# One of four weight sums of a seven-product multiplication moved from accumulating transfers to GpSimd, and two pieces of work swapped in the first set

## The chip, the core and the metric

One core of one Trainium2 chip runs the whole program in one launch. The metric is device time in microseconds of one execution, median of three runs.

## What is computed

A two-layer decoder trunk on 256 tokens of width 1024. Each layer has two feed-forward parts around a token mixer and a cross-attention; everything is float32:

```python
def swiglu(h, w_gate, w_up, w_down):
    return (jax.nn.silu(h @ w_gate) * (h @ w_up)) @ w_down

for i in range(DEPTH):                      # DEPTH = 2
    h = h + 0.5 * swiglu(rmsnorm(h, ffn1_norm[i]), ffn1_w_gate[i], ffn1_w_up[i], ffn1_w_down[i])
    ...                                     # mixer, cross-attention
    h = h + 0.5 * swiglu(rmsnorm(h, ffn2_norm[i]), ffn2_w_gate[i], ffn2_w_up[i], ffn2_w_down[i])
```

The gate and up matrices are 1024 x 2816, so a feed-forward part works through five and a half blocks of 512 hidden columns. The change is in the first feed-forward part of the program, `ffn1` of layer 0.

## The kernel before

**Precision.** TensorE multiplies in a reduced float32. Each weight is therefore split into a high part (`whi`, a cast on ScalarE, L224) and a low part (`wlo`, weight minus high part, a subtraction on VectorE, L225), and each block of a product is three matmuls: high by high, low by high, high by low (`mm3`, L262, L263, L264). The unit of this work is a *granule* (class `Gran`): two weight blocks of 128 rows x 512 columns, so each split is one 128x1024 instruction on ScalarE and one on VectorE. There are four buffers for high and four for low parts, so the splits can stand at most four granules ahead of TensorE. The low part is first wanted by the second matmul of its granule (L263).

**Seven products.** For some column blocks, gate and up are computed together: with B11, B21 the upper and lower 512 rows of the up block and B12, B22 those of the gate block, a 2x2 block product is done with seven block products in place of eight (`seven`). This needs sums of weights as right operands:

- X1 = B11 + B12, into a tile of its own, by VectorE (L203);
- X2 = X1 + B22, in place, by VectorE (L203, a 128x2048 addition of two SBUF tiles);
- X4 = X2 + B21, in place, by two transfers issued by GpSimd that read B21 from memory again and add it to the tile (L199);
- X3 = B12 + B22, in place over B12, before the change by two such transfers too.

The products come in the order B11, X1, X2, B22, X3, B21, X4; each is two granules of 6 matmuls (1.36 us by the spacing of the matmuls). One such run over a column block is here called a *set*. The first feed-forward part has three sets, `c` = 2, 3 and 4.

**Weaving.** Between the products stand ordinary granules of 12 matmuls (2.72 us), of the projections not done by sevens and of the down projection. A list of counts says how many of them stand ahead of each of the seven products (`share`). The loads of X2 and X3 are called for when X1's product has been issued:

```python
for w in {0: (x2, x3), 3: (x4,)}.get(i, ()):
    w.load()
```

**Order.** The order of TensorE's work is written out by the program. In the stretch at issue a scheduler orders what the other engines' queues hold; each engine then runs its queue strictly in order and waits at its head. Weight loads go through SyncE's queue into nine buffers.

Of the kernel before, what the change touches and what calls it, by code (L numbers as in the profile page):

```python
# [12 lines left out]
ALU = mybir.AluOpType  # L13
# [44 lines left out]
def trunk(ctx, tc, a, out):  # L58
    nc = tc.nc
# [15 lines left out]
    def acc(name):  # L75
        return pacc.tile([P, 512], F32, name=name, tag="acc")
# [4 lines left out]
    def work(name, n=512, dt=F32):  # L81

        return wk.tile([P, n], dt, name=name, tag="v", bufs=6) if n <= 256 else wk.tile([P, n], dt, name=name, tag="w")
# [24 lines left out]
    class Pipe:  # L108
# [4 lines left out]
        def after(self, us, f):  # L113
            self.q.append((self.t + us, f))
# [30 lines left out]
    class W:  # L145
# [6 lines left out]
        def load(self, k=None, nk=None):  # L152
            if k is None:
                if self.t is not None:
                    return
                k, nk = 0, self.nk
            if self.t is None:
                t = wp.tile([P, 2048], F32, name="w", tag="w")
                self.t = t[:, :self.nk * self.n].rearrange("p (k c) -> p k c", c=self.n)
            r0 = (self.k0 + k) * P  # L160
            nc.sync.dma_start(self.t[:, k:k + nk, :], self.src[r0:r0 + nk * P, self.c0:self.c0 + self.n]
                              .rearrange("(k p) c -> p k c", p=P))
# [17 lines left out]
    class Sum:  # L180
# [5 lines left out]
        def load(self):  # L186
            if self.t is not None:
                return
            self.l.load()
            if self.into is None:  # L190
                self.r.load()
                self.t = wp.tile([P, 2048], F32, name="w", tag="w").rearrange("p (k c) -> p k c", c=512)
            else:
                self.t = self.l.t
            w = self.r
            if self.into == "dma":
                for k in (0, 2):
                    r0 = (w.k0 + k) * P
                    nc.gpsimd.dma_start(self.t[:, k:k + 2, :], w.src[r0:r0 + 2 * P, w.c0:w.c0 + w.n]  # L199
                                        .rearrange("(k p) c -> p k c", p=P), accum_op=ALU.add)  # L200
            else:
                w.load()
                nc.vector.tensor_tensor(self.t, self.l.t, w.t, op=ALU.add)  # L203

    class Gran:

# [54 lines left out]
    def mm3(o, lh, ll, rh, rl, start, stop, onto=False):  # L261
        nc.tensor.matmul(o, lhsT=lh, rhs=rh, start=start, stop=False, skip_group_check=onto)  # L262
        nc.tensor.matmul(o, lhsT=lh, rhs=rl, start=False, stop=False, skip_group_check=onto)  # L263
        nc.tensor.matmul(o, lhsT=ll, rhs=rh, start=False, stop=stop, skip_group_check=onto)  # L264
# [93 lines left out]

    ONTO = {2: 0, 4: 0, 3: 1, 5: 1, 6: 1}

    def seven(b1, b2, x, mix, after, order=(0, 1, 2, 3, 5, 4, 6), second="dma"):

        b11, b21 = (W(b1[0], k, 4, b1[1], 512) for k in (0, 4))
        b12, b22 = (W(b2[0], k, 4, b2[1], 512) for k in (0, 4))
        x1 = Sum(b11, b12)
        x2 = Sum(x1, b22, second)
        x4 = Sum(x2, b21, "dma")
        x3 = Sum(b12, b22, "dma")
        banks = {}

        def a(t, h):
            return lambda k: tuple(v[:, t * P:(t + 1) * P] for v in pipe.need(x, 4 * h + k))

        def s(i):
            return lambda k: tuple(v[:, k * P:(k + 1) * P] for v in pipe.need(mix, i))
        plan = [(x1, s(0)), (b11, a(0, 0)), (b22, s(1)), (x2, s(2)), (b21, a(0, 1)), (x3, s(3)), (x4, a(1, 1))]
        out = []
        for i in order:
            w, lhs = plan[i]
            for k0 in (0, 2):  # L380
                def step(g, i=i, lhs=lhs, k0=k0):
                    if not k0:
                        banks[i] = banks[ONTO[i]] if i in ONTO else acc("seven")
                    for k in range(k0, k0 + 2):
                        lh, ll = lhs(k)
                        mm3(banks[i], lh, ll, g.hi[:, k - k0, :], g.lo[:, k - k0, :], k == 0 and i < 2, k == 3, onto=i in ONTO)
                        pipe.pe(0.68)
                    if k0:
                        for w in {0: (x2, x3), 3: (x4,)}.get(i, ()):
                            w.load()  # L390
                        after(i, banks)
                out.append((Gran(w.k0 + k0, 2, (w, 0, 512)), step))
        return out
# [242 lines left out]
    first_norm = nrm = Norm(cols0, mixes=True)  # L636
# [145 lines left out]
    def ffn_hidden(nm, l, norm, fin, tail, extra=None):  # L782
# [11 lines left out]
        def gate_fin(c):  # L794
            def fin(ps):
                if c == 0:
                    pipe.after(T["gate"], gated(c, ps, 512))
                else:
                    gated(c, ps, 512)()
            return fin  # L800

        def up_fin(c, o=0, n=512):
            def fin(ps):
                if o:
                    gated(c, ps, n)()
                us = box.pop(c)
                for t in range(2):
                    nc.vector.scalar_tensor_tensor(us[t][:, :n], ps[t][:, o:o + n], norm.col[:, t:t + 1], us[t][:, :n],
                                                   op0=ALU.mult, op1=ALU.mult)
                pipe.after(T["hid"], lambda: turn(c, us, n))  # L810
                extras(c)
            return fin

        def extras(c):
            for i in (2 * c, 2 * c + 1):
                if extra and i in extra:
                    extra[i]()

        def seven_fin(c):
            us, t = {}, {}  # L820

            def after(i, b):
                v = nc.vector

                def copy():
                    t[i] = work(f"p{i}")
                    nc.scalar.copy(t[i], b[i])

                def c12():
                    us[0] = t[3]  # L830
                    v.tensor_tensor(us[0], b[2], t[3], op=ALU.subtract)
                    nc.scalar.copy(b[2], t[1])
                    nc.scalar.activation(us[0], us[0], AF.Silu, scale=norm.col[:, 0:1])

                def c22():
                    us[1] = t[0]
                    v.tensor_tensor(t[0], t[0], b[5], op=ALU.subtract)
                    nc.scalar.activation(t[0], t[0], AF.Silu, scale=norm.col[:, 1:2])
                    if c == 4:
                        extras(6)  # L840

                def up(r):
                    v.scalar_tensor_tensor(us[r], b[i], norm.col[:, r:r + 1], us[r], op0=ALU.mult, op1=ALU.mult)
                    if r:
                        pipe.after(T["hid"], lambda: turn(c, [us[0], us[1]], 512))
                        extras(c)
                pipe.after(0.7, {0: copy, 1: copy, 3: copy, 2: c12, 5: c22, 4: lambda: up(0), 6: lambda: up(1)}[i])
            return after

        def turn(c, us, n):  # L850
            for i in range(0, n // P, 2):
                tp = v2(small_ps("htp"))
                for j in range(2):
                    for t in range(2):
                        nc.tensor.transpose(tp[:, j, t * P:(t + 1) * P], us[t][:, (i + j) * P:(i + j + 1) * P], ident)  # L855
                hi = v2(slot("hid_hi", F32R))
                lo = v2(slot("hid_lo", F32R))
                nc.scalar.copy(hi, tp)
                nc.vector.tensor_tensor(lo, tp, hi.bitcast(F32), op=ALU.subtract)
                for j in range(2):  # L860
                    hid[4 * c + i + j] = (hi[:, j, :], lo[:, j, :])
        wg, wu = a[nm + "_w_gate"][l], a[nm + "_w_up"][l]
        wide([(wg, 0, 512)], norm, "gate", gate_fin(0), **({} if units else dict(single=True, eng=nc.gpsimd)))
        c = HID // 512
        half = stream([(wg, c * 512, 256), (wu, c * 512, 256)], norm, "gateup", up_fin(c, 256, 256))
        five, six = [0, 1, 1, 1, 1, 0, 1], [1, 1, 1, 1, 1, 0, 1]
        if norm is first_norm:
            wide([(wu, 0, 512)], norm, "up", up_fin(0))
            n = half + stream([(wg, 512, 512)], norm, "gate", gate_fin(1)) + stream([(wu, 512, 512)], norm, "up", up_fin(1))
            counts = {2: [5, 1, 1, 1, 1, 1, 1], 3: [1, 1, 2, 1, 1, 1, 1], 4: [1, 1, 1, 1, 1, 1, 1]}  # L870
        else:
            n = stream([(wu, 0, 512)], norm, "up", up_fin(0)) + half
            counts = {1: six, 2: five, 3: six, 4: five}
# [10 lines left out]
            n += d0[i:j] + d1[i:j]  # L884
        steps = []
        for c, k in counts.items():
            s = seven((wu, c * 512), (wg, c * 512), norm.x, norm.s, seven_fin(c), (1, 0, 3, 2, 5, 4, 6), "dve")
            steps += share(n[:sum(k)], s, k)
            n = n[sum(k):]
        assert not n  # L890
# [796 lines left out]
```

## Time and profile before

| what | us |
|---|---|
| median of three runs | 1257.75 |
| range of the three | 1257.62 to 1258.05 |
| the profiled execution, its own time | 1258.38 |
| its span, first to last instruction | 1256.6 |
| TensorE busy in the span | 1247.1 (99%) |
| VectorE busy | 1057.2 (84%) |
| ScalarE busy | 873.5 (70%) |
| GpSimd busy | 162.5 (13%) |

All engines' busy time is an average over stages of the program; the first feed-forward part takes about the first 160 us. In the rows below PE is TensorE, DVE is VectorE, ACT is ScalarE, POOL is GpSimd and SP is SyncE; a q behind the engine's name marks its queue of instructions, where transfers are issued.

### The profile page before, as it was taken

What the parts mean: (1) busy time and instruction counts of PE and PEld (TensorE: products, weight loads), DVE (VectorE), ACT (ScalarE), POOL (GpSimd) and SP (SyncE); (2) the same over time, 40 slices, a digit from 0 to 9 for tenths busy, and PEclk for the clock granted to TensorE, in tenths of its full rate; (3) what the DMA queues carried; (4) which work ended last, traced back from release to release, by engine and by line L of the source; (5) the groups of instructions that cost most, each with busy time, mean ns of one, the idle gap of its engine ahead of it and who ended that gap; (6) DMA issues with size and microseconds to landing.
All of it is one profiled execution on the core that took longest, in us unless ns stands there. A gap on an engine that the chain in (4) does not pass through costs nothing.

```text
span 1256.6 us, 18186 instructions
## 1 busy us (share of the span) xinstructions
PE 1247.1 (99%) x6751; PEld 1071.7 (85%) x6751; DVE 1057.2 (84%) x1451; ACT 873.5 (70%) x1388; POOL 162.5 (13%) x139
## 2 busy tenths in 40 slices
PE   9999999999999999999999999999999999999997
PEld 7888888788998888888888889999998898888886
DVE  6998787887787999887998976798898887898886
ACT  6676764686676776767776756777876775877772
POOL 1101102101101111110111000022233100011100
PEclk9999999999999999999999999999999999999999
DMA  9989976445776688987879977665636586489961
GB/s 330 301 255 259 314 256 208 137 165 170 222 214 170 165 252 260 293 246 234 240 198 268 311 247 221 192 193 168 201 134 185 169 246 182 157 251 256 258 190 34
DMA packets 161195, 275.03 MB, mean 219 GB/s; under 512 B 7209, under 2 KB 43730, under 8 KB 161106
## 3 DMA queue, kind: packets, MB, share of 16 engines
q1 hardware_dynamic: 137744, 229.75, 53.4%
q0 software_dynamic: 19744, 38.28, 17.7%
q10 hardware_dynamic: 3618, 5.84, 1.4%
q8 instruction: 53, 0.87, 0.3%
q14 instruction: 36, 0.29, 0.1%
HBM read 271.72 MB, written 2.13 MB: 218 GB/s over the span
## 4 chain that ended last, share of the span: by engine, by line
PE 94%; DMA 2%; DVE 2%; ACT 2%; issue 1%; POOLq 0%; POOL 0%; SPq 0%; ACTq 0%; DVEq 0%
PE out L262 9%; PE out L264 9%; PE out L263 9%; PE seven L263 8%; PE seven L262 8%; PE seven L264 8%; PE htp L855 1%; PE up L263 1%; PE up L264 1%; PE up L262 1%; PE xs L264 1%; PE xs L262 1%; PE xq L263 1%; PE xq L264 1%; PE xs L263 1%; PE xq L262 1%
## 5 line engine op out<-in xcount | busy, mean ns | idle before, releaser
L225 DVE TENSOR_TENSOR wlo<-w,whi 128x1024 fp32r<-128x1024 f32 (+2 forms) x532 | 639.4, 1220 | 134.6 <-ACT whi L224 126.8
L224 ACT CAST whi<-w 128x1024 fp32r<-128x1024 f32 (+2 forms) x534 | 551.0, 1039 | 245.2 <-PE out L264 84.0
L262 PE MATMUL out<-whi,hid_hi 128*128 128x512 f32 x336 | 132.3, 394 | 0.0
L264 PE MATMUL out<-whi,hid_lo 128*128 128x512 f32 x336 | 131.0, 390 | 0.0
L263 PE MATMUL out<-wlo,hid_hi 128*128 128x512 f32 x336 | 130.8, 389 | 0.0
L263 PE MATMUL seven<-wlo,s_hi 128*128 128x512 f32 x272 | 106.0, 390 | 0.6 <-DVE wlo L225 0.6
L262 PE MATMUL seven<-whi,s_hi 128*128 128x512 f32 x272 | 106.2, 390 | 0.0
L264 PE MATMUL seven<-whi,s_lo 128*128 128x512 f32 x272 | 105.9, 389 | 0.0
L199 POOL DMA_DIRECT2D w<-in_ffn_w_up_dram x30 | 36.7, 1268 | 346.6 <-DVE wlo L225 339.5
L203 DVE TENSOR_TENSOR w<-w 128x2048 f32<-128x2048 f32 x32 | 73.2, 2287 | 2.0 <-DMA w<-in_ffn_w_gate_dram 1.5
L264 PEld LDWEIGHTS out<-whi,hid_lo 128*128 128x128 f32 x336 | 63.1, 188 | 13.4
L263 PEld LDWEIGHTS out<-wlo,hid_hi 128*128 128x128 f32 x336 | 63.1, 188 | 12.6
L262 PEld LDWEIGHTS out<-whi,hid_hi 128*128 128x128 f32 x336 | 63.1, 188 | 12.5
L262 PE MATMUL seven<-whi,xh 128*128 128x512 f32 x180 | 70.5, 392 | 0.0
L264 PE MATMUL seven<-whi,xl 128*128 128x512 f32 x180 | 70.1, 389 | 0.0
L263 PE MATMUL seven<-wlo,xh 128*128 128x512 f32 x180 | 70.0, 389 | 0.0
L263 PEld LDWEIGHTS seven<-wlo,s_hi 128*128 128x128 f32 x272 | 51.1, 188 | 11.4 <-DVE wlo L225 1.0
L264 PEld LDWEIGHTS seven<-whi,s_lo 128*128 128x128 f32 x272 | 51.1, 188 | 10.7
L262 PEld LDWEIGHTS seven<-whi,s_hi 128*128 128x128 f32 x272 | 51.1, 188 | 10.4
L199 POOL DMA_DIRECT2D w<-in_ffn_w_gate_dram x30 | 36.9, 1467 | 176.2 <-DVE xst L1146 62.3
L264 PEld LDWEIGHTS seven<-whi,xl 128*128 128x128 f32 x180 | 33.8, 188 | 7.1
L262 PEld LDWEIGHTS seven<-whi,xh 128*128 128x128 f32 x180 | 33.8, 188 | 6.8
(395 smaller groups left out, 3013.7 us busy)
## 6 DMA issues: line engine op xcount, KB each, us to landing
w<-in_ffn_w_up_dram SPq DMA_DIRECT2D x40, 1024.0 KB, 7.8
w<-in_ffn_w_down_dram SPq DMA_DIRECT2D x40, 1024.0 KB, 9.3
w<-in_ffn_w_gate_dram SPq DMA_DIRECT2D x38, 1024.0 KB, 8.9
w<-in_ssd_w_in_dram SPq DMA_DIRECT2D x24, 1024.0 KB, 5.4
w<-in_xa_w_kv_dram SPq DMA_DIRECT2D x16, 1024.0 KB, 6.4
w<-in_ffn_w_gate_dram POOLq DMA_DIRECT2D x30, 512.0 KB, 9.7
w<-in_ffn_w_up_dram POOLq DMA_DIRECT2D x30, 512.0 KB, 7.2
w<-in_da_w_in_dram SPq DMA_DIRECT2D x12, 1024.0 KB, 5.2
```

Of the source, the lines that this page charges most:

```text
L199: nc.gpsimd.dma_start(self.t[:, k:k + 2, :], w.src[r0:r0 + 2 * P, w.c0:w.c0 + w.n] .rearrange("(k p) c -> p k c", p=P), accum_op=ALU.add)
L203: nc.vector.tensor_tensor(self.t, self.l.t, w.t, op=ALU.add)
L224: nc.scalar.copy(hv, src)
L225: self.eng.tensor_tensor(self.lo[:, :, o:o + n], src, hv.bitcast(F32), op=ALU.subtract)
L262: nc.tensor.matmul(o, lhsT=lh, rhs=rh, start=start, stop=False, skip_group_check=onto)
L263: nc.tensor.matmul(o, lhsT=lh, rhs=rl, start=False, stop=False, skip_group_check=onto)
L264: nc.tensor.matmul(o, lhsT=ll, rhs=rh, start=False, stop=stop, skip_group_check=onto)
L855: nc.tensor.transpose(tp[:, j, t * P:(t + 1) * P], us[t][:, (i + j) * P:(i + j + 1) * P], ident)
```

## The change

In the first feed-forward part alone, X3 is no longer made by two accumulating transfers but by GpSimd: four additions of 128x512, each of two SBUF tiles, B12 plus B22. For that, B22 is read from the tile in which it lies anyway. In the first set, two ordinary granules in place of one stand ahead of X2's product, and none in place of one ahead of B21's. The number of products and of ordinary granules is the same.

```diff
@@ class Sum, load
             else:
                 w.load()
-                nc.vector.tensor_tensor(self.t, self.l.t, w.t, op=ALU.add)
+                if self.into != "pool":
+                    nc.vector.tensor_tensor(self.t, self.l.t, w.t, op=ALU.add)
+                    return
+                for k in range(4):
+                    nc.gpsimd.tensor_tensor(self.t[:, k, :], self.t[:, k, :], w.t[:, k, :], op=ALU.add)
@@ seven
-        x3 = Sum(b12, b22, "dma")
+        x3 = Sum(b12, b22, third)
@@ ffn_hidden
-            counts = {2: [5, 1, 1, 1, 1, 1, 1], 3: [1, 1, 2, 1, 1, 1, 1], 4: [1, 1, 1, 1, 1, 1, 1]}
+            counts = {2: [5, 1, 2, 1, 1, 0, 1], 3: [1, 1, 2, 1, 1, 1, 1], 4: [1, 1, 1, 1, 1, 1, 1]}
...
-            s = seven((wu, c * 512), (wg, c * 512), norm.x, norm.s, seven_fin(c), (1, 0, 3, 2, 5, 4, 6), "dve")
+            s = seven((wu, c * 512), (wg, c * 512), norm.x, norm.s, seven_fin(c), (1, 0, 3, 2, 5, 4, 6), "dve",
+                      "pool" if norm is first_norm else "dma")
```

On GpSimd, in the three sets of the first feed-forward part, the queue before holds X3's transfers (target `w_584`, `w_882`, `w_1230`, the tiles of B12) and X4's (target the tile of X1 and X2):

```order
L199 DMA w_584<-in_ffn1_w_gate_dram 128x2x512 x2
L199 DMA w_586<-in_ffn1_w_up_dram 128x2x512 x2
L199 DMA w_882<-in_ffn1_w_gate_dram 128x2x512 x2
L199 DMA w_884<-in_ffn1_w_up_dram 128x2x512 x2
L199 DMA w_1230<-in_ffn1_w_gate_dram 128x2x512 x2
L199 DMA w_1232<-in_ffn1_w_up_dram 128x2x512 x2
```

The same place of the changed program (`w_637`, `w_975`, `w_1295` are the tiles of B22):

```order
L207 TENSOR_TENSOR w_584<-w_584,w_637 128x512 x4
L199 DMA w_586<-in_ffn1_w_up_dram 128x2x512 x2
L207 TENSOR_TENSOR w_884<-w_884,w_975 128x512 x4
L199 DMA w_886<-in_ffn1_w_up_dram 128x2x512 x2
L207 TENSOR_TENSOR w_1234<-w_1234,w_1295 128x512 x4
L199 DMA w_1236<-in_ffn1_w_up_dram 128x2x512 x2
```

Six transfers have become twelve additions, in the same places of the queue.

On VectorE around the first set's X2, before: the X1 sum (`w_586<-w_522,w_584`), X1's two low parts, one of an ordinary granule (`w_616`), the X2 sum, X2's two low parts:

```order
L203 TENSOR_TENSOR w_586<-w_522,w_584 128x2048
L859 TENSOR_TENSOR hid_lo_576<-htp_570,hid_hi_575 128x512
L225 TENSOR_TENSOR wlo_583<-w_586,whi_582 128x1024
L225 TENSOR_TENSOR wlo_597<-w_586,whi_596 128x1024
L225 TENSOR_TENSOR wlo_615<-w_616,whi_614 128x1024
L203 TENSOR_TENSOR w_586<-w_586,w_629 128x2048
L225 TENSOR_TENSOR wlo_628<-w_586,whi_627 128x1024
L225 TENSOR_TENSOR wlo_643<-w_586,whi_642 128x1024
```

The same place of the changed program:

```order
L204 TENSOR_TENSOR w_586<-w_522,w_584 128x2048
L863 TENSOR_TENSOR hid_lo_576<-htp_570,hid_hi_575 128x512
L229 TENSOR_TENSOR wlo_583<-w_586,whi_582 128x1024
L229 TENSOR_TENSOR wlo_597<-w_586,whi_596 128x1024
L229 TENSOR_TENSOR wlo_615<-w_616,whi_614 128x1024
L229 TENSOR_TENSOR wlo_628<-w_616,whi_627 128x1024
L204 TENSOR_TENSOR w_586<-w_586,w_637 128x2048
L229 TENSOR_TENSOR wlo_645<-w_586,whi_644 128x1024
```

The second ordinary granule's low part has come ahead of the X2 sum, which is now one instruction later.

On VectorE in the second set of the changed program, from the low part of the last ordinary granule of the first set (`w_789`) over the X1 sum (`w_886<-w_840,w_884`) and X1's first low part to the last evacuation ahead of the X2 sum; `p`, `gs` and `hid_lo` instructions each have one operand in PSUM:

```order
L229 TENSOR_TENSOR wlo_829<-w_789,whi_828 128x1024
L204 TENSOR_TENSOR w_886<-w_840,w_884 128x2048
L229 TENSOR_TENSOR wlo_839<-w_840,whi_838 128x1024
L229 TENSOR_TENSOR wlo_851<-w_840,whi_850 128x1024
L847 SCALAR_TENSOR_TENSOR p0_654<-seven_566,rcol_295,p0_654 128x512
L812 SCALAR_TENSOR_TENSOR gs_678<-up_710,rcol_295,gs_678 128x512
L812 SCALAR_TENSOR_TENSOR gs_679<-up_711,rcol_295,gs_679 128x512
L229 TENSOR_TENSOR wlo_870<-w_871,whi_869 128x1024
L229 TENSOR_TENSOR wlo_883<-w_886,whi_882 128x1024
```

Before, this X1 sum stood four instructions further up, ahead of X4's two low parts; the X2 sum, which stood between X1's low parts and the next ordinary granule's, now stands behind that granule's low part and four evacuations. SyncE's queue holds the same transfers in the same order as before, and so does the third set's VectorE queue.

## Rows read from the trace of the kernel before

**Rows 1.** Waits of TensorE, whole span: total us, times, longest.

```profile
PE warm L597 <- DVE warm L99: 1.5, 1, 1.5
PE seven L263 <- DVE wlo L225: 0.6, 1, 0.6
PE acs L1285 <- PE mk L264: 0.2, 1, 0.2
```

**Rows 2.** Busy us of each engine by stretch of the first part.

```profile
55.00:60.00 5.00, 4.37 (x20) 3.30 (x19) 3.83 (x4) 4.43 (x5) 1.58 (x2) 1.00 0.97 179
sum 137.00, PE 136.37 PEld 112.88 DVE 117.97 ACT 94.32 POOL 16.85; mean PE 27.27 PEld 22.58 DVE 23.59 ACT 18.86 POOL 3.37
```

**Rows 3.** Timeline of TensorE in the first set: start us, duration us.

```profile
51.70 0.39 PE L263 MATMUL seven<-wlo,s_hi 128*128 128x512 f32 x1
...
53.06 0.39 PE L263 MATMUL seven<-wlo,s_hi 128*128 128x512 f32 x1
...
54.42 0.39 PE L263 MATMUL gate<-wlo,xh 128*128 128x512 f32 x1
...
56.92 0.39 PE L262 MATMUL seven<-whi,s_hi 128*128 128x512 f32 x1
57.93 0.50 PE L263 MATMUL seven<-wlo,s_hi 128*128 128x512 f32 x1 [0.63 <-DVE wlo L225]
```

**Rows 4.** Timeline of VectorE in the first set.

```profile
46.22 2.29 DVE L203 TENSOR_TENSOR w<-w 128x2048 f32<-128x2048 f32 x1
48.42 0.68 DVE L859 TENSOR_TENSOR hid_lo<-htp,hid_hi 128x512 fp32r<-128x512 f32 x1
49.68 3.60 DVE L225 TENSOR_TENSOR wlo<-w,whi 128x1024 fp32r<-128x1024 f32 x3 [0.58 <-ACT whi L224]
53.20 2.28 DVE L203 TENSOR_TENSOR w<-w 128x2048 f32<-128x2048 f32 x1
56.66 6.90 DVE L225 TENSOR_TENSOR wlo<-w,whi 128x1024 fp32r<-128x1024 f32 x6 [1.17 <-ACT whi L224]
```

**Rows 5.** Timeline of ScalarE behind the first set's X2 sum.

```profile
55.57 4.88 ACT L224 CAST whi<-w 128x1024 fp32r<-128x1024 f32 x5 [0.59 <-DVE w L203]
```

**Rows 6.** Timeline of GpSimd: the first set's X3 transfers.

```profile
48.82 2.61 POOL L199 DMA_DIRECT2D w<-in_ffn_w_gate_dram  x2 [27.51 <-DVE w L203]
```

**Rows 7.** First set's B22: its issue on SyncE, and us to landing.

```profile
24.98 3.46 SPq L161 DMA_DIRECT2D w<-in_ffn_w_gate_dram  x1
w<-in_ffn_w_gate_dram SPq DMA_DIRECT2D x1, 1024.0 KB, 15.0
```

**Rows 8.** Timelines of GpSimd and VectorE, additions and low parts together and apart.

```profile
11.01 1.29 POOL L225 TENSOR_TENSOR wlo<-w,whi 128x512 fp32r<-128x512 f32 x1 [7.00 <-ACT whi L224]
...
122.62 3.48 DVE L225 TENSOR_TENSOR wlo<-w,whi 128x1024 fp32r<-128x1024 f32 x3
...
205.54 2.14 POOL L930 TENSOR_TENSOR rt<-rt,rt 128x512 f32<-128x512 f32 x1 [1.89 <-DVE rt L929]
205.32 1.21 DVE L225 TENSOR_TENSOR wlo<-w,whi 128x1024 fp32r<-128x1024 f32 x1
...
244.87 3.53 POOL L930 TENSOR_TENSOR rt<-rt,rt 128x512 f32<-128x512 f32 x2 [12.35 <-DVE rt L929]
245.54 0.41 DVE L929 TENSOR_TENSOR rt<-k,cossinr 128x256 f32<-128x256 f32 x1
245.87 4.74 DVE L225 TENSOR_TENSOR wlo<-w,whi 128x1024 fp32r<-128x1024 f32 x3
```

**Rows 9.** Second set: two rows of VectorE, one of TensorE.

```profile
79.50 1.21 DVE L225 TENSOR_TENSOR wlo<-w,whi 128x1024 fp32r<-128x1024 f32 x1
93.42 4.62 DVE L225 TENSOR_TENSOR wlo<-w,whi 128x1024 fp32r<-128x1024 f32 x4
97.96 0.39 PE L263 MATMUL out<-wlo,hid_hi 128*128 128x512 f32 x1
```

**Rows 10.** Third set: two rows of VectorE, two of TensorE.

```profile
115.00 2.35 DVE L225 TENSOR_TENSOR wlo<-w,whi 128x1024 fp32r<-128x1024 f32 x2
117.86 1.22 DVE L225 TENSOR_TENSOR wlo<-w,whi 128x1024 fp32r<-128x1024 f32 x1
118.36 0.39 PE L263 MATMUL seven<-wlo,xh 128*128 128x512 f32 x1
119.72 0.39 PE L263 MATMUL out<-wlo,hid_hi 128*128 128x512 f32 x1
```

More of the change, by code (lines that the diff above doesn't have):

```diff
@@ L359, in trunk, with seven @@
     ONTO = {2: 0, 4: 0, 3: 1, 5: 1, 6: 1}
-    def seven(b1, b2, x, mix, after, order=(0, 1, 2, 3, 5, 4, 6), second="dma"):
+    def seven(b1, b2, x, mix, after, order=(0, 1, 2, 3, 5, 4, 6), second="dma", third="dma"):
         b11, b21 = (W(b1[0], k, 4, b1[1], 512) for k in (0, 4))
```

## The prediction

> **What bounds the kernel now.** I read the waits of TensorE first, because TensorE is busy 99% of the span. Over the whole program it waits three times: at the start, 0.2 us late in the program, and 0.6 us for one low part in a seven-product set [rows 1]. The busy times by stretch then say where that is: between 20 and 157 us TensorE misses 0.63 us of 137, all of it between 55 and 60 us [rows 2]. The reader should take two things from this. The first part of the program has no more than about 0.7 us to give. And a delay that reaches TensorE there is paid in full, since nothing later waits that could absorb it.
>
> The timeline shows that one wait closely. X2's first matmul starts at 56.92, the next wants the low part 0.23 later, at 57.15, and gets it at 57.93: 0.78 lost [rows 3]. VectorE had made X1's two low parts and one ordinary one until 53.28, then the X2 sum until 55.48 [rows 4]. ScalarE's cast follows [rows 5], and the low part ends at 57.88, 2.40 behind the sum. So VectorE is what TensorE nearly waits for. It runs its low parts only about a microsecond ahead here: they end at 50.9, 52.1 and 53.3 [rows 4], and are wanted at 51.70, 53.06 and 54.42 [rows 3]. Around it VectorE is the loaded engine (118 of 137 us [rows 2]). I therefore ask of each part of the change what it does to VectorE.
>
> **The transfers taken out.** Six transfers of 512 KB go. No wait of TensorE ends on a transfer [rows 1], so I put their gain at nothing; the bound on the other side is the 0.78 us, since nothing else is idle. What covers them is the distance of four granules that the splits can run ahead.
>
> **The extra granule ahead of X2.** It gives X2 2.72 us more, and VectorE spends 1.2 of it on that granule's low part. With nothing else changed, the sum would end at 56.6, X2's low part at 59.0, and it would be wanted at 57.15 + 2.72 = 59.87. The wait goes: -0.78. The granule taken from ahead of B21 costs nothing by itself: TensorE's work is the same, and no wait stood there [rows 1].
>
> **The twelve additions.** They are new work for an idle engine, but VectorE's low parts and GpSimd's additions, both with two operands in SBUF, exclude each other in this trace [rows 8]. An addition alone takes 1.29. One that starts 0.2 behind a low part's start takes 2.14: it ends 1.15 after the low part (206.53 to 207.68). Three low parts in a row take 3.48; beside two additions they take 4.74. Taken apart: the first addition runs from 244.87 to about 246.1, a low part follows, the second addition ends at 248.40, the next low part 1.1 later. They take turns, one addition between two low parts, 1.15 + 1.1 a pair. An instruction of VectorE with an operand in PSUM is not held up (0.41 for the 128x256 one at 245.54, inside the first addition).
>
> The Trainium skill, page "SBUF — State Buffer", section "Who interferes with whom", states this as a rule: a VectorE instruction with two SBUF inputs and a GpSimd instruction that reads SBUF share a port that is held for a whole instruction. By that rule, which the turns above bear out, the additions are not free here.
>
> *First set.* GpSimd's first addition needs the X1 sum (its place in the queue was released by that sum before too, 48.8 [rows 6]) and B22, which landed at 24.98 + 15.0 = 40 [rows 7]. So it runs from 48.65 to 49.94, and from there in turns:
>
> - low part 1 of X1 ends 51.0, wanted 51.70: in time;
> - addition 52.15, low part 2 at 53.3, wanted 53.06: TensorE 0.25 late;
> - addition 54.45, the ordinary granule's low part 55.55, wanted 54.42 + 0.25: 1.15 late in all;
> - addition 56.7, the second ordinary low part 57.8, wanted 54.42 + 2.72 + 1.15 = 58.3: in time;
> - X2 sum to 60.05, X2's low part 2.40 later at 62.45, wanted 59.87 + 1.15 = 61.0: 2.6 late in all.
>
> The 2.6 stands in place of 0.78: **+1.8**. Bounds: -0.78 if the additions hold nothing up; +2.4 if each takes its full 1.29 in its turn.
>
> *Second set.* The X1 sum now stands behind the low part that was made at 79.50 to 80.71 [rows 9]. With TensorE about 1.8 later, and ScalarE's casts with it (they wait for buffers), that is near 82; the sum ends at 84.2 and four additions follow. By the queue shown above, VectorE then has two low parts, three PSUM evacuations (2 us together), two low parts. One addition fits beside the evacuations with half of the next; the others hold up a low part each: some 3 us. VectorE has no idle time to recover it in before the X2 sum. The tightest low part is now the one behind the X2 sum: before, it was the second of four that start at 93.42 (ends 95.77) and was wanted at 97.96 [rows 9], a lead of 2.2, less an estimated 0.4 because the X1 sum comes later. 3.0 against 1.8 loses 1.2, and the ordinary low part behind the evacuations a little more: I take **+1.4**. Bounds: 0, if the evacuations hide two additions; 2.8, if all four hold a low part up.
>
> *Third set.* Two low parts follow the X1 sum until 117.35, wanted at 118.36 for the second; the next ends 119.08, wanted 119.72 [rows 10]. Leads of 1.0 and 0.6 meet additions of 1.15 each; one half is covered by a PSUM instruction between them. I take **+1.1**; bounds 0 and 2.6.
>
> **Sum.** 1.8 + 1.4 + 1.1 = +4.3 us on the profiled execution's 1258.38, so 1262.7. That execution stands 0.63 above the median of the runs, so the median becomes 1262.0. The lower bounds give -0.78, 1257.0; the upper ones 2.4 + 2.8 + 2.6 = +7.8, 1265.5.
>
> The Trainium skill, page "GPSIMD Engine Reference", section "Elementwise — side-by-side cycle accounting", puts a two-input element at 2.6 cycles, which at its 1.2 GHz makes an estimated 1.11 us for 512 elements. With that price in place of 1.29 the same walk would lose about 2.5 us, 1260.2. The row (1.29) decides here.
>
> **Rivals.** About 0.2%, 2.5 us, is what a measurement of this kernel tells from no change.
>
> *No collision that counts.* For it: VectorE has idle time in the part (19 us of 137), ScalarE sets its pace at several places, and the additions could fall there. Then the extra granule's gain is left: 1258.38 - 0.78 - 0.63 = 1257.0. Against it: the first four additions start where the leads are 0.8 to 1.1 us. It decides if the first set's low parts lose less than about 0.2 us an addition.
>
> *Partly hidden.* VectorE may take two turns running, or later leads may swallow more: +0.3 to +2.4, 1258.0 to 1260.2. For it: the second set has a lead of 2.2 us [rows 9], and GpSimd spends some time between additions.
>
> *Transfers count after all.* 3 MB less traffic lets every load land earlier. It could not give more than the 0.78 us, so it ends with the first rival; a faster result needs a gain outside this part, for which I see nothing.
>
> *B22's tile held longer.* The additions read it, so its release could hold back a weight load. The first four end at 56.7; B22's own low parts are the fourth and fifth of the six that run from 56.66 to 63.6 [rows 4], and release it later anyway: no effect.
>
> *Worse than the upper bound.* X2 later makes X4's transfers later; if they miss X4's cast, another wait opens: above 1265, little chance, as eight granule times of 2.72 us lie between X2's product and X4's.
>
> **How the numbers follow.** Forecast, +2.5 to +7.2 us: 0.62. Partly hidden: 0.18. No collision: 0.11. Worse: 0.06. Faster by over 0.2%: 0.03. Slower by over 0.2% is 0.62 + 0.06 = 0.68; within it 0.18 + 0.11 = 0.29. The range takes the forecast and the partly hidden case, 1257.9 to 1265.0, some 0.80 together; the forecast's own is 1260.3 to 1265.0.
>
> **What would show it.** In the changed profile the additions should take 1.3 alone and 2.2 in turns, and low parts from 49 to 57 us 2.2 each in place of 1.2. TensorE should wait for low parts (`wlo`) 2 to 3 us in all around 53 to 62 us, and about 1 us each near 100 and 120 to 130; the stretch to 157 us should be longer by the whole difference, and everything later equal. The wait at 57.9 for X2 should be a longer one at about 61, not gone. The forecast is wrong if low parts stay at 1.2 us beside additions, if TensorE shows no wait in the first part, or if later stages change.

## The result, and the profile after

The changed kernel takes 1264.64 us (median of 6 runs, 1264.26 to 1265.38), the kernel before 1257.85 beside it (6 runs, 1257.62 to 1258.11). The ratio is 1.0054, 95% interval 1.0041 to 1.0067: 6.8 us slower, where 4.3 were forecast; the time lies in the forecast's own range of 1260.3 to 1265.0, close to its upper end. The profiled execution took 1265.38 with a span of 1263.6, 7.0 more than before.

The waits of TensorE over the whole span (total us, times, longest) answer to [rows 1]; the 1.5 us at the start and the 0.2 late in the program are as they were, and left out here:

```profile
PE seven L267 <- DVE wlo L229: 2.7, 2, 1.9
PE gate L267 <- DVE wlo L229: 0.6, 1, 0.6
PE out L267 <- DVE wlo L229: 0.2, 1, 0.2
PE xt L539 <- DMA h<-in_x_dram: 0.2, 1, 0.2
```

They are all on low parts, but for 0.2 at the start. The low parts make 3.5 us where they made 0.6 before; the rest of the 7.0 has to be found elsewhere. So I compared the start of each matmul with that of the same matmul before.

**First set.** The timelines of the changed kernel, first GpSimd, then VectorE, then TensorE, and the durations of VectorE's low parts between 49 and 57 us (ns, min/median/max):

```profile
49.05 7.99 POOL L207 TENSOR_TENSOR w<-w 128x512 f32<-128x512 f32 x4 [27.84 <-DVE w L204]
```

```profile
50.15 7.98 DVE L229 TENSOR_TENSOR wlo<-w,whi 128x1024 fp32r<-128x1024 f32 x4 [0.57 <-ACT whi L228]
58.05 2.28 DVE L204 TENSOR_TENSOR w<-w 128x2048 f32<-128x2048 f32 x1
61.50 3.50 DVE L229 TENSOR_TENSOR wlo<-w,whi 128x1024 fp32r<-128x1024 f32 x3 [1.18 <-ACT whi L228]
```

```profile
52.19 0.39 PE L267 MATMUL seven<-wlo,s_hi 128*128 128x512 f32 x1
...
55.96 0.49 PE L267 MATMUL gate<-wlo,xh 128*128 128x512 f32 x1 [0.56 <-DVE wlo L229]
...
62.78 0.50 PE L267 MATMUL seven<-wlo,s_hi 128*128 128x512 f32 x1 [0.76 <-DVE wlo L229]
```

```profile
L229 DVE TENSOR_TENSOR wlo<-w,whi x4: 1291/2302/2316, 50.1 to 55.8; 128x1024 fp32r<-128x1024 f32 x4
```

This is the walk of the prediction almost to the tenth: the four low parts end at 58.1 (57.8 forecast), one addition between two of them. The first takes 1.3, the other three 2.3 each in place of 1.2. TensorE enters the set 0.49 behind [rows 3] (52.19 for 51.70, a later start of the program) and X2's second matmul, which stands one granule of 2.72 later now, is 62.78 - 57.93 - 2.72 = 2.13 behind. The set costs 1.64.

**Second set.** The X2 sum and X4's transfers of the kernel before:

```profile
89.42 2.28 DVE L203 TENSOR_TENSOR w<-w 128x2048 f32<-128x2048 f32 x1
97.20 2.46 POOL L199 DMA_DIRECT2D w<-in_ffn_w_up_dram  x2 [17.50 <-DVE wlo L225]
```

Of the changed kernel, VectorE, GpSimd (its four additions, then X4's transfers, and the additions' durations over the program) and one matmul of TensorE:

```profile
88.56 3.83 DVE L229 TENSOR_TENSOR wlo<-w,whi 128x1024 fp32r<-128x1024 f32 x2
92.32 1.27 DVE L863 TENSOR_TENSOR hid_lo<-htp,hid_hi 128x512 fp32r<-128x512 f32 x2
93.51 2.34 DVE L229 TENSOR_TENSOR wlo<-w,whi 128x1024 fp32r<-128x1024 f32 x2
...
96.98 2.28 DVE L204 TENSOR_TENSOR w<-w 128x2048 f32<-128x2048 f32 x1
```

```profile
84.54 9.02 POOL L207 TENSOR_TENSOR w<-w 128x512 f32<-128x512 f32 x4 [18.57 <-DVE w L204]
102.20 2.42 POOL L199 DMA_DIRECT2D w<-in_ffn_w_up_dram  x2 [8.64 <-issue]
```

```profile
L207 POOL TENSOR_TENSOR w<-w x12: 1297/2271/3279, 49.1 to 127.2; 128x512 f32<-128x512 f32 x12
```

```profile
100.45 0.50 PE L267 MATMUL out<-wlo,hid_hi 128*128 128x512 f32 x1 [0.17 <-DVE wlo L229]
```

TensorE loses only 0.4 here (2.61 behind from 101 us on; 97.96 became 100.45 [rows 9]). VectorE took two turns running against the first addition, which lasted 3.28 (84.54 to 87.82, over two low parts of 1.21 each). But the X2 sum starts at 96.98, where it started at 89.42 before, and the transfers that follow X2's low parts are issued from 102.20 on in place of 97.20.

**Third set.** Of the kernel before, SyncE's load of B12 and B22 and VectorE's X1 sum:

```profile
104.36 5.81 SPq L161 DMA_DIRECT2D w<-in_ffn_w_gate_dram  x2
112.79 2.29 DVE L203 TENSOR_TENSOR w<-w 128x2048 f32<-128x2048 f32 x1 [1.28 <-DMA w<-in_ffn_w_gate_dram]
```

Of the changed kernel, the same load, VectorE, TensorE, and the busy times of the engines by stretch (PE, PEld, DVE, ACT, POOL, then the granted clock, the DMA share, GB/s):

```profile
107.01 5.82 SPq L161 DMA_DIRECT2D w<-in_ffn_w_gate_dram  x2
```

```profile
118.20 2.29 DVE L204 TENSOR_TENSOR w<-w 128x2048 f32<-128x2048 f32 x1 [4.04 <-DMA w<-in_ffn_w_gate_dram]
120.41 3.44 DVE L229 TENSOR_TENSOR wlo<-w,whi 128x1024 fp32r<-128x1024 f32 x2
123.78 0.68 DVE L841 TENSOR_TENSOR p<-p,seven 128x512 f32<-128x512 f32 x1
124.37 6.17 DVE L229 TENSOR_TENSOR wlo<-w,whi 128x1024 fp32r<-128x1024 f32 x3
```

```profile
121.68 0.50 PE L267 MATMUL seven<-wlo,xh 128*128 128x512 f32 x1 [1.90 <-DVE wlo L229]
...
126.33 0.40 PE L267 MATMUL out<-wlo,hid_hi 128*128 128x512 f32 x1
```

```profile
120.00:122.00 2.00, 0.32 (x1) 0.30 (x2) 2.00 (x3) 0.00 (x0) 1.07 (x1) 1.00 0.82 304
122.00:124.00 2.00, 1.98 (x7) 1.05 (x5) 2.00 (x2) 0.00 (x0) 2.00 (x2) 0.64 0.03 13
124.00:126.00 2.00, 2.00 (x5) 1.63 (x6) 2.00 (x2) 1.51 (x2) 2.00 (x2) 0.51 0.51 53
```

The X1 sum waited 4.04 us for B12's load, 1.28 before: it starts at 118.20 and not at 112.79, 5.41 later, though the load was issued only 2.65 later, about as much as TensorE is. TensorE then waits 1.90 for X1's low part, and behind that wait its granted clock is 0.64 and 0.51, at or near the lower of its two levels, until 126 us: this part of the loss is in no wait. The matmul at 119.72 of [rows 10] starts at 126.33, 6.61 later, and by 135 us TensorE is 7.37 behind. The third set costs 7.37 - 2.61 = 4.76: by the starts of the matmuls 2.2 by the end of the wait, 1.8 in the stretch of the lower clock up to 126.1, 0.8 behind it. (0.3 of it comes back near 815 us, which the change does not touch.) Start 0.5, first set 1.6 to 1.7, second 0.4, third 4.8: the third set is where the forecast, 1.1, was far off.

My theory after this reading: the additions' turns cost the first set what was said; in the third set a second thing is added, B12's late landing, because X4's transfers start 5 us later and run into it. Rivals: the order with the granule moved costs by itself; the third set's loss is its own additions; B12 is late because SyncE issues it late.

### The profile page after: what moved, and what is told of

Same layout as the page of the kernel before. It is cut to its first block, busy times and chain, and to the rows that moved or that the text cites. A ratio compares the mean times of both kernels' runs of the same rounds, so it can differ in the third digit from the quotient of the medians.

```text
span 1263.6 us, 18184 instructions
## 1 busy us (share of the span) xinstructions
PE 1251.4 (99%) x6751; PEld 1073.3 (85%) x6751; DVE 1065.1 (84%) x1451; ACT 873.0 (69%) x1388; POOL 180.4 (14%) x145
## 3 DMA queue, kind: packets, MB, share of 16 engines
HBM read 268.57 MB, written 2.13 MB: 214 GB/s over the span
## 4 chain that ended last, share of the span: by engine, by line
PE 94%; DVE 3%; issue 1%; DMA 1%; ACT 0%; POOLq 0%; POOL 0%; SPq 0%; DVEq 0%; ACTq 0%
PE out L267 9%; PE out L268 9%; PE out L266 8%; PE seven L267 8%; PE seven L268 8%; PE seven L266 8%; DVE wlo L229 2%; PE xs L268 2%; PE xs L266 2%; PE xs L267 2%; PE htp L859 1%; PE up L268 1%; PE up L267 1%; PE up L266 1%; PE mk L266 1%; PE mk L268 1%
## 5 line engine op out<-in xcount | busy, mean ns | idle before, releaser
L229 DVE TENSOR_TENSOR wlo<-w,whi 128x1024 fp32r<-128x1024 f32 (+2 forms) x532 | 646.8, 1234 | 130.2 <-ACT whi L228 122.0
L199 POOL DMA_DIRECT2D w<-in_ffn_w_gate_dram x24 | 29.4, 1463 | 116.6 <-DVE xst L1151 62.5
L267 PEld LDWEIGHTS seven<-wlo,xh 128*128 128x128 f32 x180 | 34.1, 189 | 10.3 <-DVE wlo L229 3.5
```

Of the source, the lines that this page charges most:

```text
L229: self.eng.tensor_tensor(self.lo[:, :, o:o + n], src, hv.bitcast(F32), op=ALU.subtract)
```

## The experiments

What "loses" means below: how much further TensorE falls behind the kernel before in that stretch of the profiled execution, from the starts of the same matmuls.

**The order alone, and the additions made short.** Three kernels. In the first, X3 comes by transfers as before and only the counts are changed; the other two edit the changed kernel.

```diff
 granule_only
-                      "pool" if norm is first_norm else "dma")
+                      "dma")
 adds_narrow
-                    nc.gpsimd.tensor_tensor(self.t[:, k, :], self.t[:, k, :], w.t[:, k, :], op=ALU.add)
+                    nc.gpsimd.tensor_tensor(self.t[:, k, :16], self.t[:, k, :16], w.t[:, k, :16], op=ALU.add)
 writes_only
-                for k in range(4):
-                    nc.gpsimd.tensor_tensor(self.t[:, k, :], self.t[:, k, :], w.t[:, k, :], op=ALU.add)
+                for k in (0, 1, 2, 3) * 2:
+                    nc.gpsimd.memset(self.t[:, k, :], 1.0)
```

> B12 + B22 by accumulating transfers as before, only the granule moved ahead of X2. Turns theory (the additions on GpSimd cost, the order gives): the 0.78 us wait before X2's second matmul goes and nothing else changes, 1257.1. Rival (the granule taken from ahead of B21 leaves B21's low part late, so the order costs by itself): a new wait of 1 to 2 us between 60 and 75 us, 1258 to 1259.

> All twelve additions stay in their places, each over 16 of 512 columns, so that X3 is mostly B12 alone (B22 is left out of the other columns). Turns theory: an addition then holds VectorE up by a tenth of a microsecond, the changed kernel's whole loss goes and the granule's gain is left, 1257.1. Rival (the loss is that of the order, the transfers left out or the tiles held longer, not of the additions' length): 1262 or more, with the B12 load near 118 us as late as in the changed kernel.

> In place of each set's four additions, eight fills of 128x512 with a constant on GpSimd, which write the same tiles and read nothing (X3 is then a constant). Theory (what the two engines take turns at is reading SBUF: VectorE's second operand and GpSimd's operands): low parts beside the fills stay at 1.2 us, the first set loses nothing and its 0.9 is gained; in all as the kernel with narrow additions or better, 1257 to 1259. Rival (any long GpSimd instruction on SBUF holds a low part up): low parts beside the fills take longer than 1.2 by up to one fill, and the first set loses again, 1260 or more.

Measured: granule_only 1258.83 (ratio 1.0005, 0.9996 to 1.0013), adds_narrow 1258.48 (1.0000, 0.9991 to 1.0009), writes_only 1257.72 (0.9997, 0.9987 to 1.0007). In all three the loss of the changed kernel is gone, so it hangs on how long GpSimd reads, and the six transfers left out are worth nothing that the times show (adds_narrow has none of them, granule_only all). The 1257.1 expected of granule_only and adds_narrow was missed all the same; writes_only came out as expected. The granule gains 0.92 in the first set of all three, and then 1.02, 2.06 and 1.53 are lost in the third, without any addition of weight there. Of granule_only, VectorE's sums and TensorE's wait:

```profile
92.60 2.27 DVE L204 TENSOR_TENSOR w<-w 128x2048 f32<-128x2048 f32 x1
...
113.54 2.29 DVE L204 TENSOR_TENSOR w<-w 128x2048 f32<-128x2048 f32 x1 [2.75 <-DMA w<-in_ffn_w_gate_dram]
```

```profile
117.02 0.50 PE L267 MATMUL seven<-wlo,xh 128*128 128x512 f32 x1 [0.57 <-DVE wlo L229]
```

The new order of granules in the first set moves VectorE's order in the second: the X2 sum starts at 92.60 where it was at 89.42, with TensorE 0.72 earlier. B12 of the third set lands later. X4's transfers start 0.40 later (97.60 for 97.20), 1.12 against TensorE. So the rival that the order costs by itself is half right: it costs, but two sets later.

The fills of writes_only took 0.52 each, from 48.23 to 52.04, over VectorE's first low parts, and those did not get longer (GpSimd, then VectorE):

```profile
48.23 3.81 POOL L207 MEMSET w<- 128x512 f32 x8 [27.23 <-DVE w L204]
```

```profile
49.34 4.75 DVE L229 TENSOR_TENSOR wlo<-w,whi 128x1024 fp32r<-128x1024 f32 x4 [0.57 <-ACT whi L228]
```

**Set by set.** The additions in some sets alone (the others by transfers), with the new order or that of before:

```diff
-                      "pool" if norm is first_norm else "dma")
 adds_set1
+                      "pool" if norm is first_norm and c == 2 else "dma")
 adds_set3
+                      "pool" if norm is first_norm and c == 4 else "dma")
 adds_sets12
+                      "pool" if norm is first_norm and c < 4 else "dma")
 adds_old_order (additions in all three sets), adds_set3_old (with c == 4)
-            counts = {2: [5, 1, 2, 1, 1, 0, 1], 3: [1, 1, 2, 1, 1, 1, 1], 4: [1, 1, 1, 1, 1, 1, 1]}
+            counts = {2: [5, 1, 1, 1, 1, 1, 1], 3: [1, 1, 2, 1, 1, 1, 1], 4: [1, 1, 1, 1, 1, 1, 1]}
```

> Order as in the changed kernel, additions on GpSimd in the first set only. Turns theory, each set pays by itself: +1.7 in the first set, nothing later, 1259.5. Rival (the third set's loss of 4.8 us comes from the delay that the earlier sets pass on, which pushes its B12 load into the transfers for X4): a further 1 to 4 us near 120 us, 1260.5 to 1263.

> Additions on GpSimd in the third set only. If the third set's 4.8 us are the turns of its own additions: 1257.1 + 4.8, about 1262. If they come from the late B12 load that the first two sets cause, and the clock behind it: B12 lands as in the kernel before, the additions cost about 1.1, 1258.2.

> Order as in the changed kernel, additions on GpSimd in the first two sets, transfers in the third. Theory (the third set's 4.8 us are two things: about 2.35 because its B12 load lands late behind the second set's X4 transfers, about 2.4 for the turns of its own additions): B12 lands near 118 as in the changed kernel, TensorE loses 2.3 us near 120, in all 2.4 less than the changed kernel, 1262.2. Rival (all of it is the late load, and the lower clock behind the wait): 1264.6. Other rival (all of it is its own additions): 1260.

> Additions on GpSimd in all three sets, granules in the order of before. Theory (the additions carry the loss, and the new order gives nothing beyond the first set, since it moves the second set's X2 sum 3.2 us later): the first set loses 2 to 3, its wait for X2 above 2; the second set's X2 sum is earlier than in the changed kernel and with it X4's transfers and the third set's B12; in all within 1.5 of the changed kernel, 1263 to 1266. Rival (order and additions add up, the order being worth its 0.9 in the first set alone): 1265.5 or more.

> Order of before, additions on GpSimd in the third set alone, so that B12 lands in time there (112.8). By the walk of the prediction the additions lose 1.1 there: 1258.9. By the kernel with additions in the third set and the new order they lose about 2.4 (4.4 less about 2.0 for a B12 that came late): 1260.2.

Measured: adds_set1 1260.80 (1.0021, 1.0013 to 1.0030); adds_set3 1260.63 (1.0019, 1.0011 to 1.0028); adds_sets12 1261.85 (1.0040, 1.0027 to 1.0052; three runs at 1261.7 to 1261.9, two at 1263.8 and 1264.8); adds_old_order 1266.46 (1.0076, 1.0063 to 1.0090); adds_set3_old 1260.35 (1.0016, 1.0007 to 1.0025).

adds_set1 loses 1.7 in the first set and 1.36 more in the third, which has no addition: each set does not pay by itself, and the time is that of the rival. adds_set3 came out between its two expectations: with the new order B12 is late there too. adds_set3_old is the clean price of the additions in the third set, since its X1 sum starts at 112.97, practically on time:

```profile
112.97 2.29 DVE L204 TENSOR_TENSOR w<-w 128x2048 f32<-128x2048 f32 x1 [1.37 <-DMA w<-in_ffn_w_gate_dram]
115.17 3.45 DVE L229 TENSOR_TENSOR wlo<-w,whi 128x1024 fp32r<-128x1024 f32 x2
118.55 0.67 DVE L841 TENSOR_TENSOR p<-p,seven 128x512 f32<-128x512 f32 x1
119.15 6.17 DVE L229 TENSOR_TENSOR wlo<-w,whi 128x1024 fp32r<-128x1024 f32 x3
```

It loses 2.04 there. The two low parts take 3.45 in place of 2.35, the next three 6.17 in place of 1.22 and 2.36 with a wait between: 3.7 us more, where the prediction counted one and a half additions of 1.15. adds_old_order is the slowest of all: without the extra granule the first set loses 3.2, the second 2.8 and the third 2.75. Its time lies above the 1263 to 1266 expected, and the reason given for them failed too: X4's transfers start at 103.63 there and the X1 sum at 119.30, both later than in the changed kernel. Against TensorE, 5.8 behind by then, that sum is only 0.7 late, so the third set pays mostly for its own additions. The rival's 1265.5 or more holds. The granule does repay part of what the additions cost. adds_sets12 came out at 1261.85, close to the 1262.2 expected, but its profiled execution (1263.78) is one with the lower clock: 0.62 and 0.52 from 122 to 126 us, behind a wait of 1.84 for X1's low part. It loses 3.8 in the third set without additions there, 2.1 by the end of that wait and 1.65 in the stretch of the lower clock:

```profile
106.35 5.82 SPq L161 DMA_DIRECT2D w<-in_ffn_w_gate_dram  x2
117.48 2.29 DVE L204 TENSOR_TENSOR w<-w 128x2048 f32<-128x2048 f32 x1 [3.97 <-DMA w<-in_ffn_w_gate_dram]
```

The 2.1 is the price of the late load alone, and near the 2.3 expected.

**How long a low part is held up.** Each addition cut into four; and X3's sum made by VectorE itself.

```diff
 adds_quarters
-                    nc.gpsimd.tensor_tensor(self.t[:, k, :], self.t[:, k, :], w.t[:, k, :], op=ALU.add)
+                    for j in range(0, 512, 128):
+                        o, b = self.t[:, k, j:j + 128], w.t[:, k, j:j + 128]
+                        nc.gpsimd.tensor_tensor(o, o, b, op=ALU.add)
 adds_vector
-                      "pool" if norm is first_norm else "dma")
+                      "dve" if norm is first_norm else "dma")
```

> The same additions, each cut into four of 128 columns. Turns theory (a low part waits for the GpSimd instruction that is running, and for no more): low parts that took 2.2 to 2.3 beside an addition take about 1.6, an estimate from 1.15 + a third of 1.29, and more of them are held up; the loss falls by a half or more, 1259.5 to 1262. Rival (the two engines share a rate, and only the sum of the elements counts): 1264.6.

> X3's sum made by VectorE, one instruction of 2.29 us a set, behind X2's sum; GpSimd adds nothing. Turns theory: four additions on GpSimd hold VectorE up by about 4 x 1.15 = 4.6 a set, so a sum that occupies VectorE itself for 2.29 costs less: 1259.5 to 1262. Rival (GpSimd's work is mostly free and the loss comes from the loads): as slow as the changed kernel or slower, 1264.6 to 1268.

Measured: adds_quarters 1262.72 (1.0040, 1.0027 to 1.0052), adds_vector 1260.94 (1.0028, 1.0018 to 1.0039). The low parts and GpSimd's additions of adds_quarters in the first set:

```profile
L231 DVE TENSOR_TENSOR wlo<-w,whi x10: 1286/1480/1494, 49.6 to 65.7; 128x1024 fp32r<-128x1024 f32 x10
```

```profile
48.46 17.66 POOL L209 TENSOR_TENSOR w<-w 128x128 f32<-128x128 f32 x16 [27.28 <-DVE w L204]
```

A low part takes 1.48 beside a quarter, 2.30 beside a whole addition: it waits for the one instruction that runs. A shared rate would have left it at 2.3. But sixteen turns stretch over 17.7 us, and the whole gains only 2, less than the half expected: the first set loses nothing now (it gains 0.2), the second 2.7 and the third 2.4. A sum on VectorE, 2.28 us of the engine that everything waits for, is cheaper than four additions on the idle one by 3.7 (1260.94 against 1264.64). In the profiled execution it loses nothing before 113 us, and 4.8 in the third set, where B12 again lands late (X1 sum at 115.38, TensorE 1.17 ahead of before): 3.1 by the end of the wait and 1.6 in a stretch of the lower clock behind it.

**B12's landing.** One kernel takes the second set's X4 transfers away, one takes the extra granule from ahead of X3 instead of B21 and has no additions.

```diff
 adds_no_x4
                 w.load()
+                if self.into == "none":
+                    return
...
-        x4 = Sum(x2, b21, "dma")
+        x4 = Sum(x2, b21, "none" if third == "pool" and b1[1] == 1536 else "dma")
 granule_from_x3
-            counts = {2: [5, 1, 2, 1, 1, 0, 1], 3: [1, 1, 2, 1, 1, 1, 1], 4: [1, 1, 1, 1, 1, 1, 1]}
+            counts = {2: [5, 1, 2, 1, 0, 1, 1], 3: [1, 1, 2, 1, 1, 1, 1], 4: [1, 1, 1, 1, 1, 1, 1]}
...
-                      "pool" if norm is first_norm else "dma")
+                      "dma")
```

> The changed kernel without the second set's two accumulating transfers for X4 (its X4 is X2 alone, B21 is left out). Theory (the third set's B12 load lands at 118.2 because those transfers start 5 us later than before and run into it): B12 lands near 114, the X1 sum starts at about 114, the wait of 1.9 and the lower clock near 122 go, and the third set pays for its own additions alone, 1.1 to 2.4 in place of 4.8: 1261 to 1262.2. Rival (B12 is late because its issue waits for low parts to release buffers): it lands near 118 as before the edit, 1264.6.

> No additions on GpSimd; the extra granule ahead of X2 is taken from ahead of X3 instead of B21, with which VectorE's order in the second set stays that of before. Theory (the granule is worth 0.9 in the first set, and loses 1.0 in the third only because the new order of VectorE in the second set makes X4's transfers and so B12 late): 0.9 better than the kernel before, 1256.9 to 1257.2, B12's landing earlier by as much as TensorE is. Rival (TensorE that is earlier by 0.9 meets B12 at the time of before anyway): no gain, within 0.3 of the kernel before.

Measured: adds_no_x4 1260.09 (1.0015, 1.0006 to 1.0023), granule_from_x3 1256.97 (0.9988, 0.9979 to 0.9997), the fastest of all kernels here. SyncE's issue and VectorE's X1 sum in adds_no_x4:

```profile
106.40 5.82 SPq L161 DMA_DIRECT2D w<-in_ffn_w_gate_dram  x2
```

```profile
113.47 2.29 DVE L206 TENSOR_TENSOR w<-w 128x2048 f32<-128x2048 f32 x1
```

B12 is issued at the same time as in adds_sets12 (106.35) and the X1 sum no longer waits for it; in adds_sets12 it started at 117.48. So it is not the issue that is late, it is the transfers ahead that hold the load up. (In the changed kernel the DMA share is 1.05 from 116 to 120 us, at 388 to 410 GB/s: the engines that move the data have nothing to spare there.) The third set then loses 0.04, additions included, and the clock stays at 1.00. That is better than the 1261 to 1262.2 expected: with B12 there early, the X1 sum starts 0.68 later than before and TensorE is 2.01 later, so VectorE is 1.3 us further ahead. That lead can pay for most of the 2.04 that the turns cost in adds_set3_old; where the other 0.7 went no run shows.

The starts side by side, from the timelines of VectorE and GpSimd (us), with what the third set loses:

| kernel | X2 sum, second set | X4's transfers | X1 sum, third set | third set loses |
|---|---|---|---|---|
| before | 89.42 | 97.20 | 112.79 | |
| granule_from_x3 | 88.22 | 96.00 | 111.21 | 0.0 |
| granule_only | 92.60 | 97.60 | 113.54 | 1.02 |
| adds_set1 | 95.13 | 100.37 | 116.42 | 1.36 |
| adds_narrow | 92.56 | 97.79 | 114.52 | 2.06 |
| adds_sets12 | 96.31 | 101.51 | 117.48 | 3.8, lower clock |
| adds_set3_old | 89.52 | 97.31 | 112.97 | 2.04, additions |
| adds_set3 | 92.13 | 97.11 | 114.04 | 4.43, additions |
| changed kernel | 96.98 | 102.20 | 118.20 | 4.76, additions, lower clock |

Wherever the transfers for X4 exist, the X1 sum starts 15.2 to 16.9 us behind their first issue (15.7 to 16.4 in the four kernels with them that are not in the table). It is 15.2 to 15.7 where VectorE's order in the second set is that of before, and 15.7 to 16.9 where it is the new one: so up to 1.3 us of the lateness is not the later start of these transfers, and its cause stays open. Taking the sum's delay against the kernel before less TensorE's own: granule_only is 0.75 + 0.72 = 1.47 late and loses 1.02, adds_set1 1.82 and 1.36, adds_narrow 2.48 and 2.06. The loss is the lateness less a lead of 0.42 to 0.46. The changed kernel is 5.41 - 2.61 = 2.80 late, which makes 2.35 of its 4.76; the other 2.4 are its additions and the lower clock together. In adds_set3, with the clock at 1.00, the same sum gives 2.0 for B12 and 2.4 for the additions, so by this sum the clock adds little to the changed kernel. Its starts agree: 2.2 are lost by the end of the wait, which is the late load, and 2.6 behind it, where the additions by themselves cost 2.04 (adds_set3_old). That leaves an estimated 0.5 for the clock. In the stretch of the lower clock the turns and the slower matmuls run side by side, so the runs do not part them more closely.

## Why the prediction was right, and where it was not

- **Additions and low parts take turns**: right. Alone 1.30, in turns 2.27; low parts 2.3 beside an addition, 1.48 beside a quarter, 1.2 beside fills. This agrees with the rule of the Trainium skill, page "SBUF — State Buffer", section "Who interferes with whom", that the shared ports are an exclusive lock, and that a VectorE instruction with two SBUF inputs contends with a GpSimd instruction that reads SBUF but not with one that only writes it.
- **First set, +1.8**: right, with its mechanism: 1.6 to 1.7.
- **Second set, +1.4**: 0.4 for TensorE. The partly hidden case (VectorE takes two turns running, the lead swallows the rest) was right for this set: one of the four additions met two low parts that were not held up. The prediction stopped there: a delay that TensorE does not feel was counted as gone. It moved on to X4's transfers.
- **Third set, +1.1, bounds 0 to 2.6**: the step that failed in size, 4.76. Its own turns cost 2.04 where B12 is on time (adds_set3_old), because the walk counted one and a half additions and the low parts there take 3.7 us longer. B12's late landing adds 2.2 to 2.35, and was not in the sum at all: the walk took the start of the X1 sum from the rows of the kernel before, where it already waited 1.28 for that load. The rival "worse than the upper bound" had the late X4 transfers, and looked for their victim in X4's cast, eight granules on; the victim was the load that moves behind them.
- **The extra granule, -0.78**: -0.92 in the first set. "The granule taken from ahead of B21 costs nothing by itself" failed: it delays the second set's X2 sum by 3.2 us and costs 1.0 in the third set. Taken from ahead of X3 it costs nothing (granule_from_x3), and TensorE has no wait left in the first part.
- **The sum**: that 1264.64 fell in the range is in part luck. The second set cost 1.0 less than its term and the third 3.7 more, 2.2 beyond its own upper bound, by a path that the prediction did not have.
- **Six transfers taken out, nothing**: right as far as the times tell (1258.48 without them in adds_narrow, 1258.83 with them in granule_only).
- **B22's tile held longer, no effect**: no run shows one; adds_narrow, where the additions hold it, and granule_only, where they do not, both issue the third set's B12 at 103.64. **Everything later equal**: within 0.3 us, and nearly all the other kernels show the same 0.3 at the same place.

## What to carry to other kernels

Before giving work to an idle engine, see whether its reads exclude those of the busy one; here 1.3 us of GpSimd cost VectorE 1.1 each, and the sum on VectorE itself cost less. Where a wait hides a delay, follow what the delayed instruction releases: here transfers that started 5 us later held up a load that the next set waits for. And when the order of one set is changed, look in the other sets at what the scheduler made of it: of two ways to move one granule, one gained 0.9 us by the matmuls' starts (1.4 by the medians) and one nothing.

## What the runs showed of the hardware that was not expected

- TensorE's granted clock fell to its lower level for some 3 to 4 us behind a single wait: to 0.64 and 0.51 behind 1.90 us (changed kernel), 0.62 and 0.52 behind 1.84 (adds_sets12), 0.50 behind 2.87 (adds_vector). In adds_narrow it waited 1.59 at the same place, and the clock stayed at 1.00. The times speak for a fall in some runs of a kernel and not in others: three of adds_vector's seven runs, 1260.38 to 1260.44, have a mean granted clock of 0.998 or 0.999, and the three from 1261.56 to 1263.35 one of 0.996 or 0.997.
- An addition of GpSimd can lose two turns running: 3.28 us, two low parts of VectorE, in place of 1.30.
- A load of 1 MB that was issued at the same time landed at least 4 us earlier when two accumulating transfers of 512 KB ahead of it were gone (113.5 against 117.5).
